# Scheduling a one-core transformer kernel with new instruction-time estimates: a shared port for VectorE and GpSimd, and GpSimd's times by operation

## The chip, the cores and the metric

One core of one Trainium2 chip. The metric is the device time of one execution in microseconds (us). Three runs of the kernel before took 3257.03 to 3262.03 us, median 3258.47 us.

## The reference

The program applies two blocks to x (1024 tokens, width 1024, float32). The first runs a gated mixer (chunk-wise 128x128 spatial gating) and a 16-head dilated attention from one projection, merges both through gates and projects back. The second is a Mamba2 mixer, then a 16-head stick-breaking attention over shared keys and values, each followed by a per-layer embedding. What matters here are two inner loops, cut to their core:

```
# Mamba2 (ssd_chunked_scan): 4 groups of 8 heads; 8 chunks of 128 tokens, in order
acum  = cumsum(dt_k * A);  decay = exp(where(causal, acum[l] - acum[s], -inf))
y     = ((C_k @ B_k^T) * decay) @ xdt  +  (C_k @ state) * exp(acum)
state = state * exp(acum[-1]) + B_k^T @ (xdt * to_end)
# then, per group of 512 columns:  y = rms((y + D * x) * silu(z)) * y_g
# stick-breaking attention, per head and block of 128 queries
z       = q @ k^T
weights = exp(log_sigmoid(z) + suffix_sum(log_sigmoid(-z)));  o = weights @ v
```

All projections are float32 products of 1024 tokens with matrices of 1024 to 5152 columns.

## The kernel before

TensorE multiplies in a reduced float32 form, so each operand of a projection is split into a high and a low part and each product is made of three matmuls (high-high, high-low, low-high). ScalarE writes the high parts of the weights, GpSimd subtracts to get the low parts (`Gtt` with subtract, 128x1024 a piece) and multiplies gains in.

One engine's instructions run in the order in which they were written. That order comes from a builder on the host, `class Sched`. All work is written as streams, Python generators with a priority. Every helper (`A` for ScalarE, `Vtt`, `Vts`, `Vstt`, `Vcopy` for VectorE, `Gtt`, `Gts` for GpSimd, `dma`, and `mm`, `tr` for TensorE's products and transposes) emits one instruction and returns an estimate of when it ends. `op` makes the estimate: the engine's last end, or the latest dependence, plus the helper's time. `pe` advances the builder's clock `now` by TensorE's time. `run` takes the first stream in order of priority whose wait is over at `now`; lower numbers come first, 9 is the main stream of projections. So whenever the estimates say that a dependent result is not there yet, the builder writes projection matmuls into TensorE's queue; these are called filler below. Some streams (those spawned with SLACK, 1200 ns) start their steps that much later than the estimate says, so that the chip has a reserve.

```
def op(self, eng, ns, dep=0.0):
    t = max(self.e[eng], ready(dep, eng) or 0.0) + ns
    self.e[eng] = t
    return At(t, eng)
```

Three places matter to the prediction.

**Mamba's scan tables** (`steps`): once the time steps are there, 32x128 products make the running sums `acum`. They depend on work of VectorE and ScalarE after the last z projection.

**Mamba's chunk steps**: for each of 4 groups and 8 chunks there is `decay` (loads `acum` by DMA, 8 VectorE tensor_scalars at L495, an exponential, a GpSimd multiply by the masked C B product), `left_` (that product, one transpose, and a mask by affine_select at L1663), `xs` (4 transposes, two VectorE multiplies from PSUM at L488, and the GpSimd multiply that gives `xe`), `rest` (the state product 128x512, eight 128x64 products, the product with the state) and `finish` (a multiply by z, the sum of squares by ScalarE at L1755, a one-column tensor_scalar at L495, a one-column GpSimd power, a scaling of 128x512 by VectorE at L493, and the store). `xs`, `left_` and `rest` of one chunk wait for buffers of the chunk before: `finish` gives back the y buffers. Meanwhile the main stream makes the convolution inputs and z of the next group.

**Stick-breaking attention** (`sstream`, `sig`, `keep`, `weigh`): scores on TensorE, two sigmoids on ScalarE, a scan on VectorE (L2039), a GpSimd multiply, transposes (`xs` inside `weigh`), an eviction of the transposed weights split into high and low part (ScalarE and VectorE, tile m156r), and then the products with v (`vs` inside `weigh`), 8 pairs of heads one after another with the query and gate projections of the next pair as filler.

Names in rows: psum is a bank; ident is the identity that transposes; a name like m172f or m156r is a piece of one large SBUF arena, by its offset; smalls holds one-column values.

Of the kernel before, what the change touches and what calls it, by code (L numbers as in the profile page):

```python
# [15 lines left out]
ALU = mybir.AluOpType  # L16
AX = mybir.AxisListType
PSUM = bass.MemoryType.PSUM
# [13 lines left out]

def R(ap):
    return ap.bitcast(F32R)


def at(scale, part):
# [207 lines left out]
class Sched:  # L245
# [3 lines left out]
    def __init__(self):  # L249
        self.now = 0.0  # L250
        self.e = {"A": 0.0, "V": 0.0, "G": 0.0, "D": 0.0}
        self.streams = []
        self.seq = 0
        self.tick, self.cols, self.fast = 0, 0.0, False
        self.FA, self.FV, self.FG = Idle(self, "A"), Idle(self, "V"), Idle(self, "G")
# [30 lines left out]
            self.now = max(self.now, self.due(best))  # L286
            self.step(best)

    def op(self, eng, ns, dep=0.0):
        t = max(self.e[eng], ready(dep, eng) or 0.0) + ns  # L290
        self.e[eng] = t
        return At(t, eng)

# [134 lines left out]
class Builder:  # L428
# [57 lines left out]

    def Vtt(self, out, a, b, op, dep=0.0):
        self.nc.vector.tensor_tensor(out, a, b, op=op)  # L488
        return self.s.op("V", 155 + 1.042 * out.free_size(), dep)

    def Vts(self, out, a, s1, s2, op0, op1=None, dep=0.0, fast=True):
        if op1 is None:
            self.nc.vector.tensor_scalar(out, a, s1, None, op0=op0)  # L493
        else:
            self.nc.vector.tensor_scalar(out, a, s1, s2, op0=op0, op1=op1)  # L495
        return self.s.op("V", (225 if fast else 155) + (0.52 if fast else 1.042) * out.free_size(), dep)

    def Vstt(self, out, a, s, b, op0, op1, dep=0.0):
        self.nc.vector.scalar_tensor_tensor(out, a, s, b, op0=op0, op1=op1)  # L499
        return self.s.op("V", 155 + 1.042 * out.free_size(), dep)  # L500

    def Vcopy(self, out, a, dep=0.0):
        self.nc.vector.tensor_copy(out, a)
# [1 line left out]

    def Gtt(self, out, a, b, op, dep=0.0):
        self.nc.gpsimd.tensor_tensor(out, a, b, op=op)  # L507
        return self.s.op("G", (150 if op != ALU.pow else 280) + (2.1 if op != ALU.pow else 167.0) * out.free_size(), dep)

    def Gts(self, out, a, s1, s2, op0, op1, dep=0.0):  # L510
        self.nc.gpsimd.tensor_scalar(out, a, s1, s2, op0=op0, op1=op1)
        return self.s.op("G", 160 + 0.84 * out.free_size(), dep)

    def dma(self, out, in_, dep=0.0):
        self.nc.sync.dma_start(out, in_)
# [123 lines left out]
    def rstd(self, src, n, junk, dep, eps=EPS):  # L639

        s = self.s
        r = self.sm()
        yield (dep, s.FA)
        self.nc.scalar.activation(junk, src, AF.Square, accum_out=r)
        e = s.op("A", 480 + 0.84 * src.free_size(), dep)
        yield (e, s.FV)
        e = self.Vts(r, r, 1.0 / n, eps, ALU.mult, ALU.add, e)
        yield (e, s.FG)
        return r, self.Gtt(r, r, self.mhalf[:, 0:1], ALU.pow, e)
# [715 lines left out]
    def attention1(self):  # L1365
        self.banks("012", "34", "56", "7")
        nc, a, s = self.nc, self.a, self.s
# [18 lines left out]
        def sstream():  # L1386
            for p in range(8):
                o = self.pair[p]
                for h, g in self.UNITS:
# [8 lines left out]
                    for q in range(2):  # L1398
                        i = 2 * g + q
                        n = (i + 1) * P  # L1400
                        off = (NT - 1 - i) * P
                        row = self.w_ap[u][q]
                        mx = []
                        for k0 in range(0, n, 512):
                            w = min(512, n - k0)
                            yield (self.px, o["tq", i // 4], o["tk", 0], o["tk", min(1, (n - 1) // 512)])
                            bank = self.px.get()
                            e = self.scores(bank[:, :w], o, h, i, k0, w)
                            m = self.sm()
                            nc.vector.tensor_tensor_reduce(row[:, k0:k0 + w], bank[:, :w], Tt[:, off + k0:off + k0 + w],  # L1410
                                                           1.0, -3e38, op0=ALU.add, op1=ALU.max, accum_out=m)
                            e = s.op("V", 240 + 1.042 * w, e)
                            self.px.put(bank, e)
                            mx.append(m)
                        nm = self.sm()
                        e = self.Vts(nm, mx[0], mx[-1], -1.0, ALU.max, ALU.mult, e)
                        l = self.sm()
                        nc.scalar.activation(row[:, :n], row[:, :n], AF.Exp, bias=nm, accum_out=l)  # L1418
                        e = s.op("A", 480 + 0.84 * n, e)
                        s.spawn(2.5, norm(u, q, row[:, :n], l, e))  # L1420
                    if g == 2:
                        Ts.put(Tt, e)
# [30 lines left out]
    def steps(self, x, work, ac, c_, dec, tkm):  # L1453


        nc, s = self.nc, self.s
        n = NT * 32
        e_, z, w = (work[:, i * n:(i + 1) * n] for i in (1, 2, 3))
# [37 lines left out]
        self.mm(bank[:, :n], tri, e_, True, True)  # L1496
        t = self.mm(bank[:, n:], ones, e_, True, True)
        self.acd_tok.t = self.dma(self.acd, rows, max(d))
        t1 = self.Vts(tkm[:, :, 96:128], v(bank[:, :n]), -1.0, None, ALU.mult, dep=t, fast=False)
        t1 = self.Vtt(v(z), v(bank[:, n:]), tkm[:, :, 96:128], ALU.add, t1)  # L1500
        t2 = self.A(tkm[:, :, 64:96], v(bank[:, :n]), AF.Exp, t)
        t2 = self.A(dec, v(bank[:, n:]), AF.Exp, t)
# [467 lines left out]
    def stick(self):  # L1970
# [63 lines left out]
        def keep(u, q, z, x, toks, reg):  # L2034
# [3 lines left out]
            e = max(t.t for t in toks)  # L2038
            nc.vector.tensor_tensor_scan(x[:, ::-1], x[:, ::-1], self.zero.to_broadcast([P, n]), 1.0,  # L2039
                                         op0=ALU.mult, op1=ALU.add)  # L2040
            e = s.op("V", 150 + 2.05 * n, e)
            yield (e, s.FG)
            e = self.Gtt(z[:, :n - 1], z[:, :n - 1], x[:, 1:], ALU.mult, e)
            reg.give(e)
# [217 lines left out]
```

## Time and profile before

| | |
|---|---|
| three runs | 3257.03, 3258.47, 3262.03 us |
| the profiled execution's own time | 3255.16 us |
| its span | 3253.4 us |
| TensorE busy | 3102.3 us (95%), 18830 matmuls |
| VectorE, ScalarE, GpSimd busy | 1725.7, 1404.9, 1257.3 us |
| mean granted clock of TensorE | 0.982 of full speed |

How to read it: the span is the time from the first to the last instruction in the profile; the execution's own time is 1.8 us longer. A granted clock of 1.00 means TensorE's upper level, 2.4 GHz; half of it is the lower one, 1.2 GHz, and a mean between is a stretch that had both. In a row of the timeline, what stands in brackets is the engine's idle time before the instruction and what ended it.

### The profile page before, as it was taken

Reading aid. Unit: us, or ns where it says so; the run is one execution under the profiler, and the core shown is the slowest. Engines: PE = TensorE matmul, PEld = TensorE weight load, DVE = VectorE, ACT = ScalarE, POOL = GpSimd, SP = SyncE. Lnnn points to the kernel's source line nnn. Section 1 sums busy time; section 2 is a strip of 40 time slices with the busy share of each in tenths; the row PEclk is TensorE's granted clock in tenths of the full one; section 3 lists DMA queues with packets and bytes.
Section 4 is the critical chain, followed back from the end, with each engine's and each line's share of the span. In section 5 each row is a group of like instructions: output and inputs, shape, how many; then the busy total and the mean of one; then the engine's idle time right before and its main releaser. Section 6 shows DMA issues by size and latency. Waiting matters only on the chain. (4 is left out here: it accounts for less than half of the span.)

```text
span 3253.4 us, 47763 instructions
## 1 busy us (share of the span) xinstructions
PE 3102.3 (95%) x18830; PEld 2742.4 (84%) x18830; DVE 1725.7 (53%) x3080; ACT 1404.9 (43%) x2569; POOL 1257.3 (39%) x772
## 2 busy tenths in 40 slices
PE   8999999999999999999999989999998989998999
PEld 8988888888888789987878788899977778877899
DVE  2111146667673321567676765443457776878642
ACT  4322255556564311433232323223456766776421
POOL 3332111111112433324445454643335566657750
PEclk9999999999999999999999999999998999999999
DMA  4122221212122753322434334451201111113611
GB/s 138 52 68 78 81 68 57 63 53 59 53 66 91 258 175 130 113 74 77 113 83 114 81 102 146 137 205 40 85 22 33 41 38 40 40 41 120 238 55 52
DMA packets 296052, 291.33 MB, mean 90 GB/s; under 512 B 15556, under 2 KB 252276, under 8 KB 295828
## 3 DMA queue, kind: packets, MB, share of 16 engines
q1 hardware_dynamic: 295828, 288.29, 28.7%
q8 instruction: 147, 2.41, 0.3%
q14 instruction: 77, 0.63, 0.1%
HBM read 216.80 MB, written 71.43 MB: 89 GB/s over the span
## 5 line engine op out<-in xcount | busy, mean ns | idle before, releaser
L507 POOL TENSOR_TENSOR m8r<-m0f,m8r 128x1024 fp32r<-128x1024 f32 (+1 forms) x68 | 163.4, 2403 | 473.8 <-ACT m8r L484 419.1
L507 POOL TENSOR_TENSOR m16r<-m0f,m16r 128x1024 fp32r<-128x1024 f32 x66 | 167.0, 2530 | 440.6 <-ACT m16r L484 401.6
L488 DVE TENSOR_TENSOR m156r<-psum,m156r 128x384 fp32r<-128x384 f32 (+2 forms) x376 | 223.6, 605 | 157.9 <-ACT m156r L484 155.7
L484 ACT ACTIVATE m156r<-psum 128x384 fp32r<-128x384 f32 (+2 forms) x376 | 195.9, 534 | 197.1 <-PE psum L533 184.4
L507 POOL TENSOR_TENSOR m172f<-m172f,m24f 128x127 f32<-128x127 f32 (+7 forms) x128 | 185.0, 1455 | 155.8 <-DVE m24f L2039 106.1
L507 POOL TENSOR_TENSOR m24r<-m0f,m24r 128x1024 fp32r<-128x1024 f32 x64 | 155.8, 2438 | 215.6 <-ACT m24r L484 213.1
L2039 DVE TENSOR_TENSOR_SCAN m24f<-m24f,zero 128x128 f32<-128x128 f32 (+7 forms) x128 | 222.6, 1753 | 8.4 <-ACT m24f L484 7.9
L533 PE MATMUL psum<-ident,m172f 128*128 128x128 f32 (+1 forms) x1314 | 206.4, 280 | 21.5 <-DVE m172f L493 8.5
L499 DVE SCALAR_TENSOR_TENSOR m172f<-m172f,psum 128x256 f32<-128x256 f32 (+1 forms) x112 | 59.5, 534 | 267.8 <-ACT m172f L484 221.6
L533 PEld LDWEIGHTS psum<-ident,m172f 128*128 128x128 f32 (+1 forms) x1314 | 156.9, 144 | 41.4 <-DVE m172f L493 10.2
L484 ACT ACTIVATE m192f<-psum 64x256 f32<-64x256 f32 (+2 forms) x237 | 103.8, 438 | 199.6 <-PE psum L522 128.7
L507 POOL TENSOR_TENSOR smalls<-smalls,mhalf 128x1 f32<-128x1 f32 (+1 forms) x104 | 89.5, 864 | 163.9 <-DVE smalls L495 163.1
L522 PE MATMUL psum<-m108r 128*128 128x512 f32 (+3 forms) x384 | 141.7, 371 | 6.6 <-ACT m172f L484 4.5
L484 ACT ACTIVATE m40f<-psum 128x256 f32<-128x256 f32 (+1 forms) x150 | 66.5, 444 | 181.6 <-PE psum L522 141.6
L507 POOL TENSOR_TENSOR m0f<-m0f,cols 128x1024 f32<-128x1024 f32 x64 | 132.6, 2073 | 31.0 <-DMA m0f<-in_ple_gate_dram 12.6
L493 DVE TENSOR_SCALAR m172f<-m172f,smalls 128x512 f32<-128x512 f32 (+7 forms) x160 | 130.3, 814 | 19.7 <-POOL smalls L507 14.6
L1410 DVE CUSTOM_DVE_ANT_0 m172f<-psum,m24f 128x512 f32<-128x512 f32 (+1 forms) x192 | 102.8, 554 | 65.0 <-PE psum L522 64.8
L1418 ACT ACTIVATE m172f<-m172f,smalls 128x128 f32<-128x128 f32 (+7 forms) x128 | 99.3, 776 | 82.8 <-DVE smalls L495 81.2
L522 PE MATMUL psum<-m60r,m16r 128*128 128x512 f32 x504 | 134.8, 399 | 0.0
L522 PE MATMUL psum<-m44r,m8r 128*128 128x512 f32 x504 | 133.7, 399 | 0.7 <-DVE m108r L499 0.7
L522 PE MATMUL psum<-m60r,m8r 128*128 128x512 f32 x504 | 132.3, 397 | 1.7 <-DVE m108r L499 1.7
L522 PE MATMUL psum<-m44r,m16r 128*128 128x512 f32 x504 | 133.2, 402 | 0.0
(374 smaller groups left out, 8024.5 us busy)
## 6 DMA issues: line engine op xcount, KB each, us to landing
m0f<-in_w_in_dram SPq DMA_DIRECT2D x72, 512.0 KB, 3.8
m0f<-in_m_in_dram SPq DMA_DIRECT2D x38, 512.0 KB, 4.1
m92f<-acum SPq DMA_DIRECT2D x21, 512.0 KB, 10.4
m24f<-in_alibi_dram SPq DMA_DIRECT2D x16, 512.0 KB, 4.2
zd<-m40f SPq DMA_DIRECT2D x64, 128.0 KB, 1.9
m172f<-zd SPq DMA_DIRECT2D x32, 256.0 KB, 9.8
yd<-m172f SPq DMA_DIRECT2D x32, 256.0 KB, 2.2
m0f<-in_m_out_dram SPq DMA_DIRECT2D x16, 512.0 KB
```

The lines of the kernel that those rows point to most:

```text
L484: self.nc.scalar.activation(out, in_, func, **k)
L488: self.nc.vector.tensor_tensor(out, a, b, op=op)
L493: self.nc.vector.tensor_scalar(out, a, s1, None, op0=op0)
L499: self.nc.vector.scalar_tensor_tensor(out, a, s, b, op0=op0, op1=op1)
L507: self.nc.gpsimd.tensor_tensor(out, a, b, op=op)
L522: self.nc.tensor.matmul(out, l, r, start=start, stop=stop)
L533: self.nc.tensor.transpose(out, in_, self.ident[:in_.shape[0], :in_.shape[0]])
L1410: nc.vector.tensor_tensor_reduce(row[:, k0:k0 + w], bank[:, :w], Tt[:, off + k0:off + k0 + w], 1.0, -3e38, op0=ALU.add, op1=ALU.max, accum ...
L1418: nc.scalar.activation(row[:, :n], row[:, :n], AF.Exp, bias=nm, accum_out=l)
L2039: nc.vector.tensor_tensor_scan(x[:, ::-1], x[:, ::-1], self.zero.to_broadcast([P, n]), 1.0, op0=ALU.mult, op1=ALU.add)
```

## The change

No instruction is added or taken away; the estimates that the builder plans with are changed, and so the order of what it writes.

- `op` takes a flag `port`. With it, an estimate of VectorE or GpSimd may not overlap the kept intervals of the other of the two (the last 40 are kept); it starts when the later of those that it hits has ended.
- The flag is set for `Vtt` and `Vstt` when both inputs lie in SBUF, for `Vts` when output and input do, for the scan, and for all of `Gtt` and `Gts`.
- GpSimd's times: `Gtt` was 150 + 2.1 ns a column for every operation but power. It is now 190 + 2.15 for subtract and 190 + 1.77 for the others; power goes from 280 + 167 to 350 + 165; `Gts` from 160 + 0.84 to 190 + 0.84.
- `Vts` with up to 64 columns is now 155 ns; before, it was 225 + 0.52 a column.
- Four estimates of ScalarE and VectorE with sums or maxima move a little.

```diff
+def inside(*aps):
+    return all(x.space != PSUM for x in aps)
...
+        self.held = {"V": [], "G": []}
...
-    def op(self, eng, ns, dep=0.0):
-        t = max(self.e[eng], ready(dep, eng) or 0.0) + ns
+    def op(self, eng, ns, dep=0.0, port=False):
+        t = max(self.e[eng], ready(dep, eng) or 0.0)
+        if port:
+            other = self.held["G" if eng == "V" else "V"]
+            for a, b in other:
+                if t < b and a < t + ns:
+                    t = b
+            mine = self.held[eng]
+            mine.append((t, t + ns))
+            del mine[:-40]
+        t += ns
...
# Vtt and Vstt: as before, with the flag
-        return self.s.op("V", 155 + 1.042 * out.free_size(), dep)
+        return self.s.op("V", 155 + 1.042 * out.free_size(), dep, inside(a, b))
# Vts
-        return self.s.op("V", (225 if fast else 155) + (0.52 if fast else 1.042) * out.free_size(), dep)
+        if inside(out, a):
+            return self.s.op("V", 225 + 0.52 * out.free_size() if out.free_size() > 64 else 155, dep, True)
+        return self.s.op("V", 155 + 1.042 * out.free_size(), dep)
# Gtt
-        return self.s.op("G", (150 if op != ALU.pow else 280) + (2.1 if op != ALU.pow else 167.0) * out.free_size(), dep)
+        n = out.free_size()
+        return self.s.op("G", 350 + 165.0 * n if op == ALU.pow else 190 + (2.15 if op == ALU.subtract else 1.77) * n, dep, True)
# Gts
-        return self.s.op("G", 160 + 0.84 * out.free_size(), dep)
+        return self.s.op("G", 190 + 0.84 * out.free_size(), dep, True)
# the sum of squares in rstd; attention's maximum and exponential; the scan
-        e = s.op("A", 480 + 0.84 * src.free_size(), dep)
+        e = s.op("A", 366 + 0.855 * src.free_size(), dep)
-                            e = s.op("V", 240 + 1.042 * w, e)
+                            e = s.op("V", 232 + 1.05 * w, e)
-                        e = s.op("A", 480 + 0.84 * n, e)
+                        e = s.op("A", 455 + 0.855 * n, e)
-            e = s.op("V", 150 + 2.05 * n, e)
+            e = s.op("V", 125 + 2.09 * n, e, True)
```

What it moves, at three places of TensorE's queue. Lines from L504 on are the new kernel's; L541 there is L522 before (the products), L552 is L533 (the transposes).

**The scan tables.** Before: the rows with 128x512 are blocks of a projection (12 matmuls a row), the 32x128 rows are the running sums of `steps`.

```order
L522 MATMUL psum<-m16r,m156r 128x288 x6
L522 MATMUL psum<-m24r,m156r 128x288 x6
L522 MATMUL psum<-m108r,m24r 128x512 x12
L522 MATMUL psum<-m140r,m24r 128x512 x12
L522 MATMUL psum<-m108r,m24r 128x512 x12
L522 MATMUL psum<-m156r,m24r 128x512 x12
L522 MATMUL psum<-m172f 32x128 x8
L522 MATMUL psum<-m172f 128x256 x2
L522 MATMUL psum<-m108r,m8r 128x512 x12
```

Now:

```order
L541 MATMUL psum<-m24r,m156r 128x288 x6
L541 MATMUL psum<-m108r,m24r 128x512 x12
L541 MATMUL psum<-m140r,m24r 128x512 x12
L541 MATMUL psum<-m108r,m24r 128x512 x12
L541 MATMUL psum<-m156r,m24r 128x512 x12
L541 MATMUL psum<-m108r,m8r 128x512 x12
L541 MATMUL psum<-m140r,m8r 128x512 x12
L541 MATMUL psum<-m108r,m8r 128x512 x12
L541 MATMUL psum<-m156r,m8r 128x512 x12
L541 MATMUL psum<-m108r,m16r 128x512 x3
L541 MATMUL psum<-m172f 32x128 x8
L541 MATMUL psum<-m172f 128x256 x2
```

The 32x128 products stand behind 99 matmuls of 512 columns, where 48 stood before them.

**The end of mamba's first group**, chunks 6 and 7. The rows with 128x256 are filler (projections of the next group), the transposes with m44f are `xs`, the 128x512 and 128x64 rows are `rest`. Before:

```order
L522 MATMUL psum<-m24r,m108r 128x256 x9
L522 MATMUL psum<-m8r,m140r 128x256 x12
L522 MATMUL psum<-m24r,m108r 128x256 x12
L522 MATMUL psum<-m172f,m192f 128x512
L522 MATMUL psum<-m172f 128x64 x8
L522 MATMUL psum<-m192f,m76f 128x512
L533 MATMUL psum<-ident,m44f 128x128 x4
L522 MATMUL psum<-m8r,m156r 128x256 x12
```

Now:

```order
L541 MATMUL psum<-m8r,m156r 128x256 x12
L541 MATMUL psum<-m172f,m192f 128x512
L541 MATMUL psum<-m172f,m92f 128x64 x8
L541 MATMUL psum<-m192f,m60f 128x512
L552 MATMUL psum<-ident,m44f 128x128 x4
L541 MATMUL psum<-m60f,m76f 128x128
L552 MATMUL psum<-ident,m76f 128x128
L541 MATMUL psum<-m172f,m192f 128x512
L541 MATMUL psum<-m172f 128x64 x8
L541 MATMUL psum<-m192f,m60f 128x512
L552 MATMUL psum<-ident,m44f 128x128 x4
L541 MATMUL psum<-m172f,m92f 128x64 x8
```

Between the steps of the last chunks no filler row is left: chunk 5's `rest`, chunk 6's `xs`, a `left_` (the row of one 128x128 product, then one transpose), chunk 6's `rest`, chunk 7's `xs` and `rest` follow one another. Groups 2 and 3 read the same at their ends; the fourth has one such pair.

**Stick-breaking attention**, the third pair. The rows with ident are the transposes of weights, m156r is the transposed weights with v, m108r rows are scores, and m92r,m16r is filler. Before:

```order
L533 MATMUL psum<-ident,m172f 128x128 x3
L522 MATMUL psum<-m92r,m16r 128x512 x6
L522 MATMUL psum<-m156r 128x256 x4
L522 MATMUL psum<-m108r 128x384
L522 MATMUL psum<-m140r,m108r 128x384
```

Now:

```order
L552 MATMUL psum<-ident,m172f 128x128 x7
L541 MATMUL psum<-m108r 128x128
L541 MATMUL psum<-m140r,m108r 128x128
L541 MATMUL psum<-m156r,m140r 128x256 x4
L541 MATMUL psum<-m108r 128x256
```

Behind these transposes only scores stand, and no filler. Over all pairs, 20 of 160 such places had no projection matmul before, and 42 have none now.

## Rows read from the trace of the kernel before

**Rows 1.** The page: the span, and busy time of each engine.

```profile
span 3253.4 us, 47763 instructions
PE 3102.3 (95%) x18830; PEld 2742.4 (84%) x18830; DVE 1725.7 (53%) x3080; ACT 1404.9 (43%) x2569; POOL 1257.3 (39%) x772
```

**Rows 2.** Busy time by window, PE first, then PEclk; columns as the first line says.

```profile
core 0: us, PE busy (x) PEld busy (x) DVE busy (x) ACT busy (x) POOL busy (x), PEclk, DMA share, GB/s
1410.00:1500.00 90.00, 84.49 (x382) 69.30 (x381) 64.67 (x64) 36.84 (x52) 30.75 (x15) 0.96 0.27 67
1500.00:2130.00 630.00, 577.54 (x3685) 507.27 (x3684) 394.03 (x621) 204.95 (x360) 317.20 (x221) 0.97 0.41 115
2380.00:3010.00 630.00, 580.85 (x3212) 492.32 (x3211) 477.20 (x652) 434.11 (x824) 380.27 (x230) 0.97 0.16 47
```

**Rows 3.** The same view, two stretches inside mamba.

```profile
1680.00:1740.00 60.00, 55.01 (x346) 47.87 (x344) 39.12 (x69) 14.78 (x26) 30.94 (x23) 0.91 0.35 93
1830.00:1890.00 60.00, 52.98 (x292) 45.43 (x291) 45.88 (x71) 19.51 (x34) 30.52 (x20) 0.89 0.33 91
```

**Rows 4.** Timeline of PE around the scan tables: start us, duration us, what.

```profile
1409.70 1.75 PE L522 MATMUL psum<-m156r,m24r 128*128 128x512 f32 x7
1416.95 5.60 PE L522 MATMUL psum<-m172f 128*32 128x128 f32 x20 [5.51 <-POOL m24r L507]
```

**Rows 5.** Waits of PE, 1500 to 2130: us in total, times, longest.

```profile
PE psum L522 <- DVE m172f L488: 14.8, 8, 3.5
PE psum L522 <- DVE m40f L499: 12.8, 7, 3.3
PE psum L522 <- POOL m172f L507: 10.8, 7, 2.7
```

**Rows 6.** Timeline of DVE and POOL, mamba: start us, duration us, what.

```profile
1561.14 0.48 DVE L493 TENSOR_SCALAR m172f<-m172f,smalls 128x512 f32<-128x512 f32 x1
1583.61 2.51 POOL L507 TENSOR_TENSOR m16r<-m0f,m16r 128x1024 fp32r<-128x1024 f32 x1
1583.77 0.41 DVE L499 SCALAR_TENSOR_TENSOR m40f<-m40f,psum 128x256 f32<-128x256 f32 x1
1584.10 2.30 DVE L493 TENSOR_SCALAR m172f<-m172f,smalls 128x512 f32<-128x512 f32 x1
```

**Rows 7.** Groups by form, VectorE, 1500 to 2100: count, busy us, mean ns, idle before and releaser.

```profile
L493 DVE TENSOR_SCALAR m172f<-m172f,smalls 128x512 f32<-128x512 f32 x30 | 43.4, 1448 | 14.5 <-POOL smalls L507 13.9
L488 DVE TENSOR_TENSOR m172f<-psum,m92f 128x512 f32<-128x512 f32 x57 | 38.8, 686 | 27.1 <-PE psum L533 22.1 <-PE psum L522 5.0
L495 DVE TENSOR_SCALAR smalls<-smalls 128x1 f32<-128x1 f32 x30 | 4.4, 147 | 6.2 <-ACT m172f L1755 6.0
```

**Rows 8.** The same: GpSimd, whole program; ScalarE (last row), 1500 to 2100.

```profile
L507 POOL TENSOR_TENSOR m8r<-m0f,m8r 128x1024 fp32r<-128x1024 f32 x67 | 161.3, 2408 | 472.6 <-ACT m8r L484 417.9 <-PE psum L533 52.4 <-PE psum L522 1.8
L507 POOL TENSOR_TENSOR smalls<-smalls,mhalf 128x1 f32<-128x1 f32 x88 | 60.5, 691 | 149.7 <-DVE smalls L495 149.6
L507 POOL TENSOR_TENSOR m172f<-m172f 128x512 f32<-128x512 f32 x44 | 56.6, 1287 | 152.1 <-DVE m172f L488 105.0 <-DVE smalls L495 23.6 <-DVE m172f L499 14.5
L507 POOL TENSOR_TENSOR m172f<-m172f,m92f 128x512 f32<-128x512 f32 x28 | 32.2, 1149 | 47.2 <-DVE m172f L488 36.6 <-PE psum L522 10.6
L1663 POOL TENSOR_SCALAR_AFFINE_SELECT m192f<-m192f 128x128 f32<-128x128 f32 x32 | 10.6, 333 | 4.3 <-ACT m192f L484 4.2
L1755 ACT ACTIVATE m172f<-m172f 128x512 f32<-128x512 f32 x30 | 18.7, 623 | 9.0 <-DVE m172f L488 9.0
```

**Rows 9.** Waits of PE, 2380 to 3010 (stick-breaking attention).

```profile
PE psum L522 <- DVE m192f L488: 14.4, 8, 4.8
PE psum L522 <- DVE m156r L488: 13.2, 13, 2.1
PE psum L533 <- DVE m192f L488: 2.9, 2, 1.7
PE psum L522 <- ACT m156r L484: 2.4, 2, 1.8
```

More of the change, by code (lines that the diff above doesn't have):

```diff
@@ L488, in Vtt, with Vts @@
         self.nc.vector.tensor_tensor(out, a, b, op=op)
-        return self.s.op("V", 155 + 1.042 * out.free_size(), dep)
-    def Vts(self, out, a, s1, s2, op0, op1=None, dep=0.0, fast=True):
+        return self.s.op("V", 155 + 1.042 * out.free_size(), dep, inside(a, b))
+    def Vts(self, out, a, s1, s2, op0, op1=None, dep=0.0):
         if op1 is None:
@@ L495, in Vts @@
             self.nc.vector.tensor_scalar(out, a, s1, s2, op0=op0, op1=op1)
-        return self.s.op("V", (225 if fast else 155) + (0.52 if fast else 1.042) * out.free_size(), dep)
+        if inside(out, a):
+            return self.s.op("V", 225 + 0.52 * out.free_size() if out.free_size() > 64 else 155, dep, True)
+        return self.s.op("V", 155 + 1.042 * out.free_size(), dep)
     def Vstt(self, out, a, s, b, op0, op1, dep=0.0):
         self.nc.vector.scalar_tensor_tensor(out, a, s, b, op0=op0, op1=op1)
-        return self.s.op("V", 155 + 1.042 * out.free_size(), dep)
+        return self.s.op("V", 155 + 1.042 * out.free_size(), dep, inside(a, b))
     def Vcopy(self, out, a, dep=0.0):
@@ L1498, in steps @@
         self.acd_tok.t = self.dma(self.acd, rows, max(d))
-        t1 = self.Vts(tkm[:, :, 96:128], v(bank[:, :n]), -1.0, None, ALU.mult, dep=t, fast=False)
+        t1 = self.Vts(tkm[:, :, 96:128], v(bank[:, :n]), -1.0, None, ALU.mult, dep=t)
         t1 = self.Vtt(v(z), v(bank[:, n:]), tkm[:, :, 96:128], ALU.add, t1)
```

## Prediction

> **What bounds the kernel now.** I read the page first: TensorE is busy 3102.3 of 3253.4 us [rows 1], so at most 151 us stand beside it, and no order of the work can win more than these and what the clock loses. The table of windows says where they lie: 52.5 us without a matmul in mamba's stretch of 630 us, 49.2 us in the stretch of the same length with the stick-breaking attention, and 5.5 us of the 90 around the scan tables [rows 2]. The granted clock is 0.97 in both long stretches: 630 x 0.03 = 18.9 us of lower level in each, if every column at half clock costs itself once more; 0.96 in the 90 us, 3.6 us. Then the waits of TensorE in mamba [rows 5] and in the stick stretch [rows 9] name what ended the idle time. Last come the groups by form, for the duration of each link of a chain [rows 7, 8]. The reader is to see that TensorE's own work is fixed, and that the change can act only through the order: filler that stands in front of a dependent matmul hides its wait; filler that doesn't leaves the chain bare.
>
> **That the estimates now tell something true.** A VectorE scaling of 128x512 took 0.48 us alone; one that began at 1584.10, while GpSimd's subtract ran from 1583.61 for 2.51 us, took 2.30 and ended 0.28 us behind it [rows 6]. Over mamba such scalings have a mean of 1448 ns [rows 7], three times the 0.48. An operation that reads PSUM is not held: 0.41 us under the same subtract [rows 6]. GpSimd's multiply with a broadcast operand and its add differ too, 1149 and 1287 ns for 512 columns, and its subtract of 1024 takes 2408 [rows 8], as the new formulas have it (190 + 1.77 x 512 = 1096; 190 + 2.15 x 1024 = 2392). So the old plan was early at VectorE by up to 2 us in places, and chains stood bare there. One detail of the change does not agree with the rows: it also keeps one-column tensor_scalars off the port, and these took 147 ns on average over 30 [rows 7], so none can have waited out a subtract. The Trainium skill (SBUF — State Buffer, "Who interferes with whom") counts tensor_scalar among the operations that can take the shared pair and then block fully; by it each of these could have taken some 2 us, and the plan that holds them off would win their chains. By the rows it wins nothing there and makes the planned end of `finish` late. Nothing below uses the skill's value.
>
> **Part 1, the scan tables: a gain of 9.1 us.** The 32x128 products waited 5.51 us at 1416.95 behind seven matmuls that took 1.75 us, 0.25 each [rows 4]. The change puts 51 more matmuls ahead of them (99 for 48): 51 x 0.25 = 12.7 us of filler, over twice the wait. The 5.51 go, and with them the half clock behind the stop, 3.6 us. What is late next: the tables themselves, by 12.7 - 5.5 = 7.2 us; the first chunk step comes only behind 1500, so this is covered by the convolutions' filler, at the cost of nothing. Ends: 5.5 (the clock stays low for another reason) to 9.1.
>
> **Part 2, mamba's chunk steps: a gain of 1.6 us, from two large terms.** What goes: in the middle of the groups there is now filler ahead of the products that waited for GpSimd's m172f (10.8 us), of the projection blocks that waited for m40f (12.8), and of half of the `left_` products that waited for VectorE's m172f (14.8 / 2 = 7.4) [rows 5]: 31.0. Of the clock's 18.9 us, two stretches of 60 us at 0.91 and 0.89 hold 60 x 0.09 + 60 x 0.11 = 12.0 [rows 3], and the stops there are of the kind that goes; I take 15, between 12.0 and 18.9. Together 46.0.
> What comes: at the ends of the first three groups two steps follow one another without filler, and at the end of the fourth one does. The first such stop is the chain behind a subtract that has just started: subtract 2.41, mask 0.33, the add to y 1.29, `xe` 1.15 [rows 8], 5.2 us, less 1.2 us of TensorE's own work beside it, 4.0. The second is `finish` ahead of the next `xs`, since the y buffers come free only with its store: two reads of PSUM 0.69 each [rows 7], add 1.29, multiply by z 0.68, squares 0.62, tensor_scalar 0.15, power 0.69 [rows 7, 8], scaling 0.48 [rows 6] and the multiply of the next `xs` 0.69: 6.0 us, less 0.6 for transposes and products beside it, 5.4. Each group end of 4.0 + 5.4 = 9.4 us I charge with the clock price that the stop in part 1 had, 3.6: 13.0. Three times 13.0 and 5.4 for the last group make 44.4. Net -1.6. Ends: the group ends at half of it (-22, the subtracts fall elsewhere and `finish` is quick) or at 1.5 times (+22).
>
> **Part 3, the stick stretch: a loss of 0.4 us.** Places where a unit's transposes and its products follow with no projection matmul between go from 20 to 42 of 160. Each of the 20 cost, on average, (13.2 + 2.4) / 20 = 0.78 us, from the waits for m156r [rows 9]; 22 more cost 17.2. What goes by the port's being planned: half of the waits for m192f, (14.4 + 2.9) / 2 = 8.65 [rows 9], and half of the other 16.3 us of this stretch's idle time (49.2 less 14.4, 13.2, 2.9 and 2.4), 8.15. Ends of the price of a place: nothing, where a score beside it covers the eviction (the part is then -16.8), and 2.1, the longest of these waits [rows 9] (then +29.4); I take the mean, since the old places are of the same shape.
>
> **The rest at nothing.** In the first block, the gemms of per-layer embedding and the tail, order changes too, but TensorE's rows there have filler on both sides: the remaining 44 us of idle time (151 less 52.5, 49.2 and 5.5) I leave as they are, with 10 us to either side. DMA issues on SP's queue keep their neighbours, apart from the loads of `acum`, which are issued with the chunk steps.
>
> **Sum.** -9.1 - 1.6 + 0.4 = -10.3 us. The profiled execution took 3255.16, 3.3 us below the median: 3244.9 in its terms, about **3248 us** as a median.
>
> **The rivals.**
> *Faster by much.* The group ends cost half, because filler written ahead lets VectorE run ahead so that `finish` is done when TensorE arrives, and the 22 places are covered by scores. Then part 1 gives 9.1, part 2 46.0 - 22.2 = 23.8 and part 3 16.8: 49.7, near 3209. For it: VectorE is idle 47% of the span and GpSimd 61% [rows 1]. Against: the order has these steps bare, whatever stands ahead. Chance 0.12.
> *Slower, by bare places.* A plan that is late everywhere spends filler too soon: SLACK is still added to estimates that now hold the lock's wait. Each of the 22 places in the stick stretch then waits as long as the longest one did, 2.1 us [rows 9]: 46.2 - 16.8 = +29.4; with -9.1 and -1.6 from the others +18.7, near 3277; with the group ends a fifth dearer near 3286. It decides from a price of a place of 1.1 us up (22 x 1.1 = 24 = 16.8 + 7). For it: the count of bare places doubled. Against: the mean of the old ones is 0.78. The port is also reserved in the order in which instructions are written down. The chip gave it to the one that started first, the subtract of 1583.61 [rows 6]; so a plan by writing order names the wrong loser at times, and the chain that truly loses has no filler. The Trainium skill's section says the same, that issue order decides who blocks. Chance 0.26.
> *It does not do what it says.* The waits only move: what VectorE no longer waits for at one row it waits for at the next, since the lock's total time is the same and the streams' order among themselves hardly changes. 3258 within 5. Chance 0.12.
>
> **How the numbers follow.** The forecast, an exchange of waits with a small gain, has 0.50 and its own range 3233 to 3264. A measurement can tell about 0.2%, 6.5 us, from no change. Of the forecast's half, 0.29 falls below 3252, 0.12 within and 0.09 above. With the first rival 0.12, faster is 0.41; with the second 0.26, slower is 0.35; the third's 0.12 and the forecast's middle make 0.24. The range runs to the other cases on both sides until about a tenth is left out at each end: 3216 to 3285.
>
> **What would show it.** Right: no stop over 1 us ahead of the 32x128 products; waits of TensorE for GpSimd's m172f and for m40f in mamba below 5 us in total; a pair of stops of 3 to 6 us at each of three group ends; waits for m156r of some 30 us in the stick stretch; TensorE's idle time in mamba about unchanged. Wrong: the waits for m156r at 40 us or more (the second rival), or group ends under 5 us together (the first).

## The result and the profile after

The changed kernel took 3378.82 us (median of 4 runs, 3372.92 to 3388.69) beside 3257.75 us (4 runs) before: ratio 1.0372, 95% interval 1.0345 to 1.0399. It is 121 us slower. The page of the profile, the two lines that answer to [rows 1]:

```profile
span 3378.6 us, 47764 instructions
PE 3131.6 (93%) x18830; PEld 2766.9 (82%) x18830; DVE 1691.9 (50%) x3080; ACT 1408.4 (42%) x2569; POOL 1263.8 (37%) x772
```

The span is 125.2 us longer. TensorE is busy 29.3 us longer with the same 18830 matmuls, at a mean granted clock of 0.960 where it was 0.982, and idle for 95.9 us more. VectorE's busy time is less than before.

Where the idle time lies is read from the table of windows, which divides each kernel at the same five events, to a whole us: the first 32x128 product of the scan tables, the end of the third mamba group's last `rest` product, the same of the fourth group, the first score of the stick-breaking attention, and its last weighted product. The columns are those of [rows 2]: length, then busy time of TensorE with its count, the other engines, PEclk. The kernel before:

```profile
0.00:1417.00 1417.00, 1383.00 (x7739) 1206.03 (x7740) 588.60 (x1393) 586.72 (x1058) 336.63 (x191) 0.99 0.29 94
1417.00:1930.00 513.00, 481.01 (x2762) 411.78 (x2763) 348.42 (x504) 171.93 (x282) 238.06 (x160) 0.97 0.36 94
1930.00:2102.00 172.00, 158.54 (x1125) 144.05 (x1125) 88.91 (x153) 53.72 (x101) 92.24 (x64) 0.97 0.44 131
2102.00:2407.00 305.00, 296.15 (x2273) 284.55 (x2271) 127.01 (x216) 102.67 (x178) 114.38 (x66) 1.00 0.30 100
2407.00:3064.00 657.00, 607.67 (x3516) 522.68 (x3515) 498.23 (x675) 454.39 (x878) 408.92 (x246) 0.97 0.20 62
3064.00:3253.00 189.00, 175.91 (x1423) 173.34 (x1421) 74.55 (x142) 35.47 (x74) 67.10 (x46) 0.97 0.26 89
```

The changed kernel:

```profile
0.00:1415.00 1415.00, 1390.41 (x7791) 1213.95 (x7792) 599.75 (x1396) 591.54 (x1063) 339.58 (x191) 1.00 0.30 94
1415.00:1959.00 544.00, 482.79 (x2765) 413.51 (x2764) 326.10 (x504) 172.59 (x285) 250.02 (x164) 0.93 0.34 91
1959.00:2183.00 224.00, 163.69 (x1145) 150.09 (x1144) 90.03 (x156) 55.64 (x103) 103.33 (x68) 0.85 0.44 138
2183.00:2494.00 311.00, 291.29 (x2197) 277.41 (x2196) 114.25 (x209) 97.06 (x169) 91.67 (x58) 0.98 0.19 64
2494.00:3188.00 694.00, 632.79 (x3569) 543.15 (x3567) 491.35 (x683) 456.05 (x880) 419.35 (x253) 0.94 0.20 63
3188.00:3378.00 190.00, 170.59 (x1370) 168.83 (x1370) 70.47 (x134) 35.48 (x73) 59.83 (x40) 0.94 0.21 72
```

Length less busy time is the idle time of a stretch. It fell by 9.4 us up to the tables (34.0 to 24.6). It rose by 29.2 in mamba's first three groups (32.0 to 61.2), by 46.9 in the fourth (13.46 to 60.31), by 10.9 up to the first score, by 11.9 in the attention (49.3 to 61.2) and by 6.3 at the end. The clock column follows the idle time: in the fourth group it is 0.85 where it was 0.97.

**The tables** did what was forecast. The timeline of TensorE in the changed kernel shows the 32x128 products behind the added blocks with no stop ahead of them, where [rows 4] had one of 5.51 us; and then, in the same view, the bare ends of the first three groups:

```profile
1414.00 0.84 PE L541 MATMUL psum<-m108r,m16r 128*128 128x512 f32 x3
1414.77 3.00 PE L541 MATMUL psum<-m172f 128*32 128x128 f32 x20
...
1598.49 2.07 PE L541 MATMUL psum<-m172f,m192f 128*128 128x512 f32 x2 [5.79 <-POOL m172f L525]
1611.32 1.09 PE L541 MATMUL psum<-m172f,m92f 128*128 128x64 f32 x4 [4.79 <-DVE m172f L504]
...
1761.45 0.80 PE L541 MATMUL psum<-m76f 128*128 128x128 f32 x2 [4.76 <-DVE m172f L504]
1771.40 1.22 PE L541 MATMUL psum<-m172f,m192f 128*128 128x512 f32 x1 [8.09 <-POOL m172f L525]
...
1945.72 2.07 PE L541 MATMUL psum<-m172f,m192f 128*128 128x512 f32 x2 [11.74 <-POOL m172f L525]
```

These are the places that the order shows without filler. With the smaller stops beside them (0.94 in the second group; 1.86, 2.03 and 0.78 in the third) the three ends cost 10.6, 13.8 and 16.4 us of idle time. The stops go with the lower clock: sixteen 128x64 products took 1.89 us at 1589.12, ahead of the first stop, and 3.51 behind it at 1600.35.

**The end of mamba** is the largest single loss. The timeline of the changed kernel, VectorE, SyncE's queue, GpSimd and TensorE around it:

```profile
2119.60 0.68 DVE L504 TENSOR_TENSOR m172f<-psum,m92f 128x512 f32<-128x512 f32 x1
...
2121.23 0.75 SPq L534 DMA_DIRECT2D m172f<-hp  x1
...
2132.66 1.22 DVE L504 TENSOR_TENSOR m108f<-m108f,m172f 128x1024 f32<-128x1024 f32 x1 [11.78 <-DMA m172f<-hp]
...
2151.44 1.23 DVE L504 TENSOR_TENSOR m108f<-m108f,m172f 128x1024 f32<-128x1024 f32 x1 [3.76 <-DMA m172f<-hp]
2152.69 14.46 SPq L534 DMA_DIRECT2D m172f<-hp  x4
...
2160.80 1.23 DVE L504 TENSOR_TENSOR m108f<-m108f,m172f 128x1024 f32<-128x1024 f32 x1 [3.48 <-DMA m172f<-hp]
2165.58 1.23 DVE L504 TENSOR_TENSOR m108f<-m108f,m172f 128x1024 f32<-128x1024 f32 x1 [3.56 <-DMA m172f<-hp]
2170.27 1.23 DVE L504 TENSOR_TENSOR m108f<-m108f,m172f 128x1024 f32<-128x1024 f32 x1 [3.46 <-DMA m172f<-hp]
2171.57 1.04 POOL L525 TENSOR_TENSOR m172f<-m172f,m92f 128x512 f32<-128x512 f32 x1 [24.97 <-DVE m108f L504]
2172.57 1.04 POOL L525 TENSOR_TENSOR m200f<-m192f 128x512 f32<-128x512 f32 x1
2172.67 2.08 PE L541 MATMUL psum<-m172f,m192f 128*128 128x512 f32 x2 [53.04 <-POOL m172f L525]
```

The m108f rows belong to the next stage: the output projection's residual h gets its first half, hp, added tile by tile (`add` in `residual`), each tile loaded by DMA into a buffer. There are eight of them, the last five 4.7 us apart, because a load waits for the add before it (the add of 2151.44 ends at 2152.67, the next load is issued at 2152.69): one buffer goes round. GpSimd's row at 2171.57 is `xe` of the fourth group's chunk 6. It reads nothing that these adds write; its inputs were ready at 2120.3 (the row at 2119.60). It waits because its buffer is the one that the loads use: `xer` lies at block 188 of the arena, and `residual` takes its buffers at 184 and 188, four blocks each. So the eight loads went through the buffer at 188 one after another, ahead of the `xe` that still needed it, and `xe` starts as the last add ends. In the kernel before, the first of these adds started at 2140.45, 28 us behind the last scaling of `finish` (2112.03). Behind the stop the granted clock is still low, 0.62 from 2172 to 2200.

### The profile page after: what moved, and what is told of

Read it like the earlier page. It is cut to its first block, busy times and chain, and to the rows that moved or that the text cites. A ratio compares the mean times of both kernels' runs of the same rounds, so it can differ in the third digit from the quotient of the medians.

```text
span 3378.6 us, 47764 instructions
## 1 busy us (share of the span) xinstructions
PE 3131.6 (93%) x18830; PEld 2766.9 (82%) x18830; DVE 1691.9 (50%) x3080; ACT 1408.4 (42%) x2569; POOL 1263.8 (37%) x772
## 4 chain that ended last, share of the span: by engine, by line
PE 81%; DMA 6%; DVE 5%; POOL 2%; issue 2%; ACT 2%; SPq 0%; DVEq 0%; POOLq 0%; ACTq 0%
PE psum L541 75%; PE psum L552 6%; DMA m92f<-acum 2%; DVE m24f L2058 1%; DMA m172f<-hp 1%; DVE m156r L504 1%; DMA m172f<-acum 1%; POOL m172f L525 0%; DVE m172f L509 0%; DMA m108f<-hd 0%; DVE m172f L504 0%; DMA m172f<-zd 0%; DVE m108f L504 0%; DMA m192f<-ya 0%; ACT m108r L500 0%
## 5 line engine op out<-in xcount | busy, mean ns | idle before, releaser
L525 POOL TENSOR_TENSOR m8r<-m0f,m8r 128x1024 fp32r<-128x1024 f32 (+1 forms) x71 | 172.8, 2434 | 552.9 <-ACT m8r L500 515.5
L504 DVE TENSOR_TENSOR m156r<-psum,m156r 128x384 fp32r<-128x384 f32 (+2 forms) x376 | 223.0, 604 | 124.5 <-ACT m156r L500 122.3
L552 PE MATMUL psum<-ident,m172f 128*128 128x128 f32 (+1 forms) x1314 | 212.9, 287 | 26.2 <-DVE m156r L504 13.8
L2058 DVE TENSOR_TENSOR_SCAN m24f<-m24f,zero 128x128 f32<-128x128 f32 (+7 forms) x128 | 213.9, 1682 | 12.8 <-ACT m24f L500 11.7
L552 PEld LDWEIGHTS psum<-ident,m172f 128*128 128x128 f32 (+1 forms) x1314 | 161.1, 147 | 47.7 <-DVE m156r L504 16.0
L541 PE MATMUL psum<-m108r 128*128 128x512 f32 (+3 forms) x384 | 143.9, 377 | 8.4 <-ACT m172f L500 7.9
L509 DVE TENSOR_SCALAR m172f<-m172f,smalls 128x512 f32<-128x512 f32 (+7 forms) x160 | 139.2, 870 | 19.4 <-POOL smalls L525 14.8
L541 PE MATMUL psum<-m44r,m8r 128*128 128x512 f32 x528 | 139.6, 396 | 0.0
L541 PE MATMUL psum<-m44r,m16r 128*128 128x512 f32 x504 | 137.3, 407 | 0.8 <-DVE m108r L517 0.8
L541 PE MATMUL psum<-m76r,m8r 128*128 128x512 f32 x528 | 136.0, 396 | 0.0
L541 PE MATMUL psum<-m60r,m8r 128*128 128x512 f32 x528 | 135.7, 395 | 0.0
```

The lines of the kernel that those rows point to most:

```text
L541: self.nc.tensor.matmul(out, l, r, start=start, stop=stop)
L552: self.nc.tensor.transpose(out, in_, self.ident[:in_.shape[0], :in_.shape[0]])
```

## The experiments

Three theories were set against each other first. A: the port in the estimates makes dependent steps late in the plan, so that filler is spent early. B: the new times by operation moved the order. C: the order was fitted to the old estimates, and any move costs.

**The change without the port** (`if port:` becomes `if False:`).

> The change without the shared port: op never moves an estimate behind the other engine's, the new times of GpSimd and the four others stay. Theory A (the port in the estimates makes the dependent steps late in the plan, so filler is spent early and chains stand bare): the 53.0 us stop of TensorE at 2172.7 of the change and the stops of 5 to 12 us at the group ends are gone, time 3235 to 3280, within 25 us of the kernel before. Theory B (the new times by operation moved the order): the loss stays, 3340 to 3400. Theory C (the order was fitted to the old estimates, and any move of them costs): 3290 to 3330, some 30 to 70 us over the kernel before.

3250.13 us (10 runs) beside 3254.54, ratio 0.9985 (0.9975 to 0.9995). B falls, and so does C as a law: new times alone move rows as well and gain 4 us. Of A's stops none is left; the longest between the tables and the first score is 5.1 us. The stop of 5.51 us ahead of the tables is still there, so it is the port that puts filler before it. The new times change the stages even so: TensorE was idle 14.2 us less up to the tables, 10.7 more in mamba's first three groups and 7.6 less in the attention.

**The port with the old times** (all formulas as before, the flag as in the change).

> The old times of every operation, with the shared port in the estimates. Theory A (the port does it): 3350 to 3400, nearly the change's 3379, with stops of several us at the ends of mamba's groups. Theory B (the new times do it): 3245 to 3275, as before. Theory C (any move costs): 3290 to 3330.

3354.78 us (one run), with a stop of 49.83 us at the end of mamba behind the same `xe`. A holds: the port alone makes 100 of the 121 us.

**The residual's loads held back.**

```diff
 # ssd, behind its loop over the groups
+            self.ssd_done.t = s.now
 # residual
             if len(srcs) == 2:
+                yield self.ssd_done
                 for t in range(NT):
```

> The change, with one wait more in the builder: the residual's second loads (hp) are not written before the last step of mamba's chunks is written, so that they can't take the buffers at 188 to 191 that these steps still need. Theory A1 (the 53.0 us stop is the eight residual loads of 4.7 us each, which hold the buffer that xe of chunk 6 waits for): the stop falls to under 15 us and the time by 30 to 55, to 3325 to 3350. Rival A2 (the chain of the last chunks is late by itself, and the loads only stand where it waits anyway): the stop stays over 40 us and the time within 10 us of the change's 3379.

3298.56 us in one run, more than was expected of it. Then the same in four runs:

> The change with the residual's second loads held back to mamba's last chunk product, timed: one look gave 3299, and the same plan held one step longer gave 3317, with 13 us of the 18 before the hold has any effect. If a look is uncertain by some 10 us: a median of 3300 to 3312. The loss that the hold takes away then is 67 to 79 of 121 us.

3310.03 us (4 runs, 3304.97 to 3315.81), ratio to before 1.0151 (1.0133 to 1.017). So 69 of the 121 us were lost at this one place; the idle time of the fourth group falls from 60.3 to 17.3 us. The timeline of TensorE in that run shows what is left of the 53.04 us stop:

```profile
2138.16 2.07 PE L541 MATMUL psum<-m172f,m192f 128*128 128x512 f32 x2 [6.61 <-POOL m172f L525]
```

**One-column tensor_scalars without the port.**

```diff
-            return self.s.op("V", 225 + 0.52 * out.free_size() if out.free_size() > 64 else 155, dep, True)
+            return self.s.op("V", 225 + 0.52 * out.free_size() if out.free_size() > 64 else 155, dep, out.free_size() > 1)
```

> The change, but one-column tensor_scalars take no part in the port (they took 147 ns on average in the trace of before, so none waited out a subtract). If their planned waits make finish late and empty the group ends: 60 us or more of the 121 come back, 3290 to 3320, and the pairs of stops at group ends are gone. If it is the large operations: within 25 us of the change's 3379.

3346.16 us, one run: 33 us came back, between the two expectations. Mamba's first three groups were idle 49.9 us in place of 61.2, so part of the late plan is theirs. The place at the end of mamba merely moved: the fourth group was idle 18.0 us in place of 60.3, and the stretch up to the first score 39.8 in place of 19.7, together 22 us less. Now the loads of hp hold up SyncE's queue, each waiting for the add before it. Behind them stands the load of y (yd, stored at 2137.26 at the latest) that the transposes of the output projection wait for:

```profile
2137.26 0.33 SPq L534 DMA_DIRECT2D yd<-m172f  x1
...
2148.47 19.00 SPq L534 DMA_DIRECT2D m172f<-hp  x5
...
2167.52 10.48 SPq L534 DMA_DIRECT2D m172f<-yd  x5
...
2173.18 1.94 PE L552 MATMUL psum<-ident,m172f 128*128 128x128 f32 x8 [31.48 <-DMA m172f<-yd]
```

**The port in one direction.** With the loads held back, first VectorE's estimates alone wait (`other = self.held["G"] if eng == "V" else []`), then GpSimd's alone (the mirror image).

> The change with the residual's second loads held back, and with the port in one direction: VectorE's estimates wait for GpSimd's intervals, GpSimd's no longer for VectorE's. Theory D (what is left of the loss, 44 us, comes from planned waits that the chip doesn't have, above all GpSimd's, whose subtracts hardly get longer in the trace, 2408 to 2434 ns on average): 25 us or more of the 44 come back, to 3250 to 3275. Rival E (it comes from VectorE's planned waits): within 12 us of 3299.

> The mirror image: GpSimd's estimates wait for VectorE's intervals, VectorE's not for GpSimd's; the residual's second loads held back. Theory D (GpSimd's planned waits are the harm): 3280 to 3310. Rival E (VectorE's are): 3245 to 3270. If each direction alone costs little (both near 3255) the harm is that an estimate is charged in both directions for one lock.

3299.31 and 3270.11 us, one run each. By the times, E is nearer than D: against 3310, 40 us come back without VectorE's planned waits and 11 without GpSimd's, and 11 is within what one plan varied by (3298.56 to 3315.81 us in five runs with the loads held back). By stages it is less plain. Mamba's first three groups are idle 33.9 us with GpSimd free and 42.5 with VectorE free, against 60.3 with both; the first of the two then loses 14.87 us at the transposes for the output projection (m172f<-yd) and 10.06 at those of the embedding. Either direction alone relieves the group ends.

**A control: the kernel before with the reserve SLACK at 1300 ns.**

> A control: the kernel before with SLACK at 1300 ns in place of 1200, a small move of the plan that says nothing about any port. Theory C (any move of the estimates away from those that the kernel was fitted to costs): 3275 or more. Else within 15 us of 3254.

3281.38 us, one run, against 3253.01: 28 us from a move of 100 ns. That is C's number. But 16.90 us of it is one row of TensorE's timeline, the same transposes as above. Two of the residual's adds (2151.60 and 2158.65) stand between the steps of the last `finish` in VectorE's queue:

```profile
2173.61 1.94 PE L533 MATMUL psum<-ident,m172f 128*128 128x128 f32 x8 [16.90 <-DMA m172f<-yd]
```

So the loads were held one step longer, until all y are stored (`yield self.yd_tok` in `residual`), in the control and in the change.

> The kernel before with the reserve at 1300 ns (3281 as it was, with one stop of 16.9 us for y ahead of the output projection) and the residual's second loads held back in the same way. Theory G: the stop goes and the time comes to 3250 to 3268, so the control's loss was the same late y and not the move of the plan as such. Theory C (any move costs): 3275 or more.

3262.97 us, one run: the time is in G's range, but the sign that G gave did not come. The stop is there with 13.18 us, and no add stands ahead of this y, in the timeline:

```profile
2154.43 0.56 POOL L507 TENSOR_TENSOR smalls<-smalls,mhalf 128x1 f32<-128x1 f32 x1
...
2155.54 0.34 SPq L515 DMA_DIRECT2D yd<-m172f  x1
...
2158.48 0.42 SPq L515 DMA_DIRECT2D m172f<-yd  x1
...
2163.49 1.94 PE L533 MATMUL psum<-ident,m172f 128*128 128x128 f32 x8 [13.18 <-DMA m172f<-yd]
2164.67 1.23 DVE L488 TENSOR_TENSOR m108f<-m108f,m172f 128x1024 f32<-128x1024 f32 x1 [9.16 <-DMA m172f<-hp]
```

Without the adds ahead of it the stop is 3.7 us shorter, no more. This y is late by its own `finish`: its power starts at 2154.43, behind a multiply of GpSimd with gains that began at 2152.58, then y is stored and loaded again. Its scaling comes 41 us behind mamba's last product, 9 in the kernel before. Whether a small move costs by itself stays open: with the loads held back 8 us of the 28 are left, in single runs.

> The change, with the residual's second loads (hp) held back until the last y of mamba is stored, one step later than in the run that held them to the last chunk product. Theory G (the adds of the residual, 4 to 5 us apart, also stand ahead of the last finish in VectorE's queue, and so delay the y that the output projection waits for): idle time of TensorE between mamba's last step and the first score from 16.5 to under 12 us, time 3285 to 3297. Rival: the adds then come late for the residual itself, 3300 or more.

3317.29 us, a miss by the time: it was expected at 3297 or below. The idle time up to the first score did fall, to 14.2 us (16.5 in the first run with the shorter hold), by less than was expected. The plans agree up to the end of mamba, where this run is already 13 us later than that first run; the timed median of the shorter hold, 3310, lies between the two. Single runs of this plan are uncertain by some 10 us (five took 3298.56 to 3315.81), and the two holds can't be told apart by them.

**The reserve with the port.** The last theory, F: SLACK, which makes the streams of `left_`, `xs` and the attention start 1200 ns behind their estimates, stood for what the old estimates lacked, among it the port; with the port in the estimates the lock is charged twice.

> The change with the residual's second loads held back and with SLACK, the reserve of 1200 ns that some streams wait on top of their estimates, at 0. Theory F (the estimates now hold the lock, and the reserve charges it twice): the group ends' stops lose half and the time comes to 3260 to 3280. Rival: the reserve also hides waits that no estimate holds (DMA landings, clock); without it new stops appear elsewhere, 3290 or more.

3247.96 us, one run, below F's range. Then in more runs with the longer hold, which at this reserve moves no instruction (in the two traces the order on each engine is the same):

> The change with the reserve at 0 and the residual's second loads held back: the plan of the run that took 3248, timed. Theory F: 3243 to 3252, faster than before by 2 to 10 us. If that one look was luck: 3255 to 3265.

3244.94 us (6 runs) beside 3255.12, ratio 0.9969 (0.9956 to 0.9981): 134 us below the change, and 10 us or 0.3% below the kernel before, clear of the interval. And the other corner, old estimates without reserve:

> The kernel before, old estimates, no port, with the reserve at 0 and the residual's second loads held back (with the reserve at 1200 that hold moves nothing in the order of before). Theory F (the reserve stands for the lock that the old estimates lack; port and reserve together charge it twice): without either the dependent products come too early and wait, 3265 or more. Rival F2 (the reserve is of no use in either plan): 3254 or less, and the port's plan without reserve owes its 3248 to the reserve alone.

3302.36 us (4 runs), ratio 1.0142 (1.0125 to 1.016). The four corners, in us: without the port 3255 with the reserve and 3302 without; with the port 3310 with the reserve and 3245 without. The loads are held back in the last three. Beside the corner that has neither, the reserve alone is worth 47 us and the port alone 57, and both together cost as much as neither. So the two stand in for each other. That the reserve stood for the lock, and not for something else that the estimates lack, is a reading and not shown. The corners with the port also have the new times; without the port these were run at the old reserve alone, where they moved the time by 4 us. Between the corners:

> The change with the reserve at 600 ns in place of 1200, nothing else. Theory F (port and reserve charge one lock twice, so the loss grows with the reserve): between the 3245 at 0 and the 3379 at 1200, 3265 to 3320, with the three group ends' idle time between 41 and 61 us. Rival (the loss at 1200 is one accident, the buffers at mamba's end, and the reserve matters little else): 3245 to 3260, or as bad as 3350 where the accident happens here too.

> The same with 300 ns. Theory F: 3250 to 3275. Rival as above: no order between 0, 300 and 600.

3278.78 us (ratio 1.0061, 1.0039 to 1.0082) and 3265.27 us (1.0021, 1.001 to 1.0032). The order 3245, 3265, 3279, 3310 is F's: the loss grows with the reserve. It holds for the whole time and not stage by stage: mamba's first three groups are idle 41.3, 54.6, 51.9 and 60.3 us. No accident with the buffers happened at 300 or 600.

Idle time of TensorE by stage, between the same events taken exactly, the last column up to the last matmul, in us:

| kernel | to the tables | groups 1 to 3 | group 4 | to the first score | attention | end |
|---|---|---|---|---|---|---|
| before | 34.0 | 32.0 | 13.5 | 8.9 | 49.3 | 8.3 |
| the change | 24.6 | 61.2 | 60.3 | 19.7 | 61.0 | 15.3 |
| port alone | 22.9 | 57.0 | 57.4 | 19.3 | 54.5 | 8.7 |
| times alone | 19.8 | 42.7 | 16.0 | 8.1 | 41.7 | 11.7 |
| change, loads held (timed) | 25.4 | 60.3 | 17.3 | 14.8 | 53.3 | 8.0 |
| change, SLACK 600 | 25.0 | 51.9 | 10.8 | 13.0 | 43.7 | 13.2 |
| change, SLACK 300 | 24.3 | 54.6 | 10.2 | 11.3 | 39.5 | 10.6 |
| change, SLACK 0 | 24.8 | 41.3 | 12.2 | 10.6 | 35.7 | 10.5 |
| before, SLACK 0 | 33.1 | 59.5 | 20.9 | 6.2 | 43.6 | 3.0 |

The windows of the fastest one, the change with SLACK at 0 (with the loads held back), show where it still loses and where it gains against the kernel before: the three groups keep 41.3 us of idle time for 32.0, the stretch up to the tables has 24.8 for 34.0, and the attention 35.7 for 49.3.

```profile
1416.00:1939.00 523.00, 481.70 (x2768) 413.90 (x2767) 327.36 (x503) 171.74 (x284) 242.80 (x164) 0.95 0.35 93
1939.00:2091.00 152.00, 139.78 (x993) 127.66 (x992) 90.11 (x151) 49.46 (x92) 85.05 (x60) 0.97 0.45 133
2091.00:2408.00 317.00, 306.43 (x2344) 294.92 (x2342) 128.27 (x216) 103.36 (x180) 111.63 (x65) 0.99 0.30 98
2408.00:3046.00 638.00, 602.33 (x3493) 520.63 (x3492) 487.39 (x674) 452.77 (x878) 409.97 (x242) 0.97 0.19 59
```

Its group ends still have the same bare stops, at about half the price, in the timeline of TensorE:

```profile
1593.30 1.45 PE L541 MATMUL psum<-m172f,m192f 128*128 128x512 f32 x2 [3.98 <-POOL m172f L525]
...
1759.63 2.08 PE L541 MATMUL psum<-m172f,m192f 128*128 128x512 f32 x2 [6.29 <-POOL m172f L525]
...
1927.11 2.08 PE L541 MATMUL psum<-m172f,m192f 128*128 128x512 f32 x2 [4.58 <-POOL m172f L525]
```

## Why the prediction was wrong, step by step

It gave 3248 us and a range to 3285; the kernel took 3379. It forecast a gain of 10 us, and the kernel lost 121.

**Part 1** held for what it named: no stop ahead of the tables, and the products behind it took 3.00 us where they had taken 5.60 [rows 4]. That the idle time up to there fell by 9.4 us, beside the 9.1 put down, is chance: 9.1 holds 3.6 for the clock, and of the 9.4 only 5.5 are this stop.

**Part 2, what goes**, held in part. It took 31.0 us of old waits as gone because filler now stood ahead of them. The waits of TensorE in the changed kernel, from the tables to the end of mamba:

```profile
PE psum L541 <- POOL m172f L525: 80.5, 5, 53.0
PE psum L541 <- DVE m172f L504: 22.2, 10, 4.8
PE psum L541 <- DVE m40f L517: 7.8, 4, 2.6
```

The five waits for GpSimd's m172f are those at the group ends (5.8, 8.1, 1.9 and 11.7) and the 53.0; in the middle of the groups none is left, so the 10.8 of [rows 5] went. Of VectorE's m172f 13.3 us stand at the three ends and 8.8 elsewhere, 6.0 less than before, where 7.4 had been put down. The waits for m40f fell by 5.0 and not by 12.8. That is about 22 of 31.0. The order shows the price: the filler that now stands in the middle of a group is missing at its end.

**Part 2, what comes**, had the right places and a price too small: two stops at each of three ends, 28.2 us of idle time forecast, 40.8 measured (10.6, 13.8, 16.4). The chains were priced by what their own links last, with one subtract ahead. At 1945.72 the stop of 11.74 us began while GpSimd was at a subtract (1933.04); behind it came a gain multiply, an add, a mask, a second subtract, the decay's multiply and a power, and only then, at 1944.63, `xe`.

**The fourth group** was put down at 5.4 us and took 46.9 more than before, 53.04 in one stop. The step that failed is the sentence that DMA issues on SP's queue keep their neighbours. The loads of hp had moved ahead of mamba's last two chunks, with eight adds in VectorE's queue, and they hold a buffer that those chunks need. The order showed this; I had read it for TensorE, at three places. Held back, 69 of the 121 us return. That is the main miss.

It is not the only one: with the buffer free the kernel still took 3310, 62 us over the forecast. In its profile (a run of 3315.81 us) TensorE is idle 33 us more than before, 28 of them in mamba's first three groups, and busy 28 us longer. So the price of bare group ends and the clock failed as well.

**Part 3** was mis-sized in all three terms. The rows of waits in the attention of the changed kernel, 2494 to 3188:

```profile
PE psum L541 <- DVE m156r L504: 18.8, 22, 3.9
PE psum L541 <- DVE m192f L504: 13.3, 8, 3.8
PE psum L541 <- ACT m156r L500: 5.8, 6, 2.3
```

Together m156r costs 24.6 us over 42 bare places, 0.59 each where 0.78 was taken: 9.0 more than before in place of 17.2. The waits for m192f, with the transposes' row, fell from 17.3 [rows 9] to 14.1, by 3.2 in place of 8.65. The remaining idle time, of which half (8.15) was to go, rose by some 6 us. The stretch lost 11.9 us of idle time, not 0.4, and its granted clock fell from 0.97 to 0.94.

**The clock.** It was to give back 3.6 and 15 and to take three times 3.6, 7.8 us on balance; TensorE's busy time grew by 29.3 us.

**The rivals.** The slower one had the right sign and a part of the right cause (a plan that is late spends filler too soon, and SLACK is added on top), and it stood at the wrong place: it priced the attention's bare places at 2.1 us each, and these became cheaper. The four corners bear out its cause, port and reserve together, for what is left once the buffer is free. The faster rival and the one of no effect fell. Neither of the two signs of being wrong came (m156r at 40 us or more, group ends under 5): the loss lay where no sign had been set.

**The one-column tensor_scalars.** The weighing said that keeping them off the port wins nothing and makes `finish` late in the plan. Without that part of the change 33 us came back in one run, and 11.3 us of idle time in the first three groups. The sign agrees. In the changed kernel one of these operations took 0.15 us beside a subtract:

```profile
1939.51 2.34 POOL L525 TENSOR_TENSOR m24r<-m0f,m24r 128x1024 fp32r<-128x1024 f32 x1
1940.16 0.15 DVE L511 TENSOR_SCALAR smalls<-smalls 128x1 f32<-128x1 f32 x1 [0.79 <-ACT m172f L1774]
```

The Trainium skill (SBUF — State Buffer, "Who interferes with whom") lets a tensor_scalar take the shared pair and block where its operands meet further conditions; no run here shows that for one column.

**The new times.** The prediction says that the new formulas have GpSimd's times as the rows do. They give the add of 512 columns 1096 ns, as they do the multiply, where [rows 8] has 1287 (the old plan 1225). The decay's multiply of 1024 columns gets 2002, where the same trace has 2564 on average (the old plan 2300).

What stays open: how the rest divides between VectorE's and GpSimd's planned waits. One run each gave 40 and 11 us of relief, with stops at the output projection mixed in that neither direction explains. Open, too, is what of the old kernel's loss at 1300 ns is due to the move itself.

## What to carry to other kernels

In a planner that orders work by estimates, a reserve in ns can stand in for costs that the estimates lack; who puts a missing cost into the estimates should lower the reserve in the same change, and time both apart and together, as the four corners here: 3255, 3302, 3310, 3245. When a plan shifts, look in every queue, DMA queues too, for work of the next stage that has overtaken the last steps of this one, and whether it can take a buffer that they still need: that was one stop of 53 us. Filler moved into one gap is missing at the end of its stage, so price both.

## What the runs showed beside

A move of 100 ns in the reserve of the old kernel, with nothing else changed, cost 28 us in one run, with 16.9 us in one stop; with the loads of hp held back 13.2 of that stop stayed. And idle time is paid twice: in the changed kernel 95.9 us more of idle time came with 29.3 us more of busy time for the same matmuls, at a granted clock of 0.85 in the stretch with the long stop.
